# A two-layer hybrid encoder: the gate products issued in attention units 8 to 73 instead of 8 to 54

## The chip, the cores and the metric

The kernel runs on one core of one Trainium2 chip. The metric is the device time of one execution in microseconds (us), the median of several runs. A core has five engines with queues of their own: PE (TensorE, matmuls; its weight loads are shown as PEld), DVE (VectorE), ACT (ScalarE), POOL (GpSimd) and SP (SyncE, which only issues DMAs here). Each executes its own instructions in order and waits on semaphores for the others.

## What is computed

Two layers of an encoder on x of 1024 tokens by 1024 channels. Cut to what matters here, one layer is:

```
u  = RMSNorm(x) ;  z = u @ w_in          # q/k/v, two latents, a rotary key, and 2048 gate logits
yA = GQA(q, k, v)                        # 8 heads, 1024 queries x 1024 keys
yB = MLA(latent q, latent kv, rotary k)  # 8 heads, keys of width 96
g  = sigmoid(z_gate + b_gate)            # g_a and g_b
m  = (g_a * (yA @ w_branch_a) + g_b * (yB @ w_branch_b)) @ w_o
x  = x + RMSNorm(m) ;  x = x + RMSNorm(relu(RMSNorm(x) @ w_up)**2 @ w_down)
```

The gate logits need only u and w_in, so their product may stand anywhere between the projection and the branches. All products are made of two or three f16 matmuls (a high and a low part of each factor).

## The kernel before

**The attention stage.** After the projections, `mixer` runs one hand-written loop over 128 units per layer (s_ = 0 to 127, and a few more to drain). A unit is one head and one block of 128 queries against all 1024 keys. Units 0 to 63 are GQA, 64 to 127 MLA. On each engine the instructions stand in the order in which the loop writes them, except on SP, whose DMAs are placed by the framework. In unit s_ the loop writes, in this order: the rest of a gate group if it can be ended (`gate_matmuls(left)`) and its evacuation (`gate_out`, ACT); `bias(s_)` (DVE, line 828: scores times a factor, with a running minimum); the "low part" operations left from the unit before (`later`); the evacuation of the last preparation product (`prep_evac`); `low(s_-3)` (DVE); for every second unit `norm` and `high` (POOL and ACT); `expo(s_)` (ACT, exponential); `scores(s_+1)` (PE); a step of the weight tasks (`advance`); the transposes of a preparation (`prep_trans`); a part of the product with v (`av_part`, line 873, 24 matmuls); the gate matmuls due (`gate_matmuls(want)`, line 673); a preparation product (`prep_mm`, 15 matmuls on lines 318 to 320, which makes q, k and v of one MLA head pair for 128 tokens); one or two more steps of the weight tasks.

**Buffers.** Scores lie in PSUM tiles A (two of them), so PE may write the scores of unit s_+1 only when `expo(s_-1)` has read its own. Everything else that PE writes in this stage lies in PSUM tiles B (four): a gate group, an `av` sum, a preparation product, transposed pieces. In SBUF there are 28 tiles "m" of 4 KB a partition (activations, results, MLA's q and k) and four tiles "w" (weights split in two).

**The gates.** There are 768 matmuls of 128x512 in 32 groups of 24, two groups for each of 16 blocks of 128 gate channels. `want` spreads them linearly over units NQ = 8 to GS = 54. A block's weights are a task of their own: a 512 KB load, a sum of squares (ACT), a matmul with ones (PE, line 243) whose result DVE copies (line 245), then the high half (POOL, line 122) and the low half (DVE, line 137). With GD = 2 the halves may be written once the gates have come within two blocks of theirs. Tasks run one after another.

**What else hangs on the numbers.** The activations U (eight tiles m) are in use as long as gates are outstanding. `PRE` says in which units the four MLA preparations run (start, step); `QS` when their weights are loaded. YA and YB hold the two branches' results in halves of two tiles m each.

Of the kernel before, what the change touches and what calls it, by code (L numbers as in the profile page):

```python
# [9 lines left out]
F16 = mybir.dt.float16  # L10
# [34 lines left out]
def tile_hybrid_encoder(  # L45
# [13 lines left out]
    V, S, G, TE, SY = nc.vector, nc.scalar, nc.gpsimd, nc.tensor, nc.sync  # L59
    depth = w_in.shape[0]  # L60
# [4 lines left out]
    dr = ctx.enter_context(tc.tile_pool(name="dr", bufs=1, space=DRAM))  # L65
# [3 lines left out]
    def nm(s):  # L69
        cnt[0] += 1  # L70
        return f"{s}_{cnt[0]}"

    def mt(shape, dt=F16):
        return sb.tile(shape, dt, tag="m", name=nm("m"), bufs=NM)
# [190 lines left out]
    def both():  # L265

        halves = []

        def alloc(shape):
            if not halves:  # L270
                t = wt([128, 2, *shape[1:]])
                halves.extend((t[:, 0], t[:, 1]))
            return halves.pop(0)
        return alloc
# [38 lines left out]
    def kview(w, k0, nk, c0, n):  # L313

        return w[k0 * 128 : (k0 + nk) * 128, c0 : c0 + n].rearrange("(k p) n -> p k n", p=128)

    def mm3(o, lh, ll, rh, rl, first, last):
        TE.matmul(o, lh, rh, start=first, stop=False)  # L318
        TE.matmul(o, lh, rl, start=False, stop=False)  # L319
        TE.matmul(o, ll, rh, start=False, stop=last)  # L320

    x1 = [dr.tile([1024, D], F32, tag=f"x1{i}", name=f"x1{i}") for i in range(depth)]
    x2 = [dr.tile([1024, D], F32, tag=f"x2{i}", name=f"x2{i}") for i in range(depth - 1)] + [out]
    gates_d = [dr.tile([16, 128, 1024], F32, tag=f"gd{i}", name=f"gd{i}") for i in range(depth)]

    def first_weights(l, res):
# [32 lines left out]
    def mixer(l, U, su_inv, b2u, w_in_, rest, late, wnext):  # L359
# [211 lines left out]
        def q_end(cb, tb):  # L571
            q_live[cb, tb] = rope_end(*q_live[cb, tb])
# [34 lines left out]
        with tc.manual_schedule(engines=ENGINES):  # L607
            pre = prelims()
            for u in range(UN):
                evac = None  # L610
                if u < 16:
                    f, tb = units[u]
# [49 lines left out]
        NGM = 32 * 24  # L662
# [24 lines left out]
        def gate_weights(nb):  # L687
            wg.append([])
            yield from wprep_steps([kview(wi, 0, 8, 1440 + nb * 128, 128)], both(), wg[nb], 1,
                                   lambda: gate_pos[0] >= 48 * (nb - GD), GP)  # L690

# [23 lines left out]
        mla, wcache, prep = {}, {}, {}  # L715
# [20 lines left out]
        def mla_qweights(i):  # L736
            w = []
            yield from wprep_steps([kview(w_q_up[l], 0, 3, i * 192, 192)], both(), w)
            (h,), (lo,), inv, f2 = w
            b2, s, iq, cq = sm(), lay(1), lay(1), lay(1)  # L740
            mul(b2, f2, bounds[2])
            yield 1
            pow2(b2, 1, s, iq)
            yield 1
            mul(cq, inv, icq)
            ts(rsc[:, i, :], rc[:, :8], cq, ALU.mult, s, ALU.mult)
            yield 1
            kap = lay(2)
            mul(kap[:, 0:1], iq, wcache["kv"][3])
            ts(kap[:, 1:2], kap[:, 0:1], -1.0 / math.sqrt(96.0), ALU.mult)  # L750
            ts(kap[:, 0:1], kap[:, 0:1], 1.0 / math.sqrt(96.0), ALU.mult)
            wcache["q", i] = (h, lo, kap)

        def prep_mm(pr, tb):
            kvh, kvl = wcache["kv"][:2]
            wqh, wql, kap = wcache["q", pr]
            if tb == 0:
                QK = {(th, hl): mt([96, 4, 512]) for th in range(2) for hl in range(2)}
                mla[pr] = (QK, mt([128, 2, 8, 128]), kap)
            th, c0 = tb // 4, (tb % 4) * 128  # L760
            pd = psD()
            for k in range(3):
                mm3(pd[:, :192], CQ[th, 0][:, k, c0 : c0 + 128], CQ[th, 1][:, k, c0 : c0 + 128],
                    wqh[:, k, :], wql[:, k, :], k == 0, k == 2)
            for k in range(2):
                mm3(pd[:, 192:448], CK[0][:, k, tb * 128 : (tb + 1) * 128], CK[1][:, k, tb * 128 : (tb + 1) * 128],
                    kvh[:, k, pr * 256 : (pr + 1) * 256], kvl[:, k, pr * 256 : (pr + 1) * 256], k == 0, k == 1)
            prep[pr, tb] = pd
# [37 lines left out]
        YA = [[mt([128, 2, 1024]) for hl in range(2)]]  # L806
        YB = []
# [10 lines left out]
        def scores(u):  # L818
            units.append(unit(u))
            pa = psA()  # L820
            units[u][0](pa)
            live[u] = pa
# [59 lines left out]
            later.append(lambda: stt(Y[pr // 2][1][:, pr % 2, q2 * 256 : (q2 + 1) * 256], pc[:, :256], 1.0 / PSC, o,  # L882
                                     ALU.mult, ALU.subtract))

        GS = 54
        TS = 3
        AL = 2
        NQ = 8
        GL = 2
        GP = True  # L890
        KVS = 36
        QS = (42, 56, 69, 86)
        GD = 2
        PRE = [(53, 1), (62, 2), (79, 1.6), (95, 1.6)]
        WN = (90, 108)
        CUT = (4, 4)
        GCUT = 2
        preps = {}
        for pr, (s0, ds) in enumerate(PRE):
            for tb in range(8):  # L900
                preps[int(s0 + tb * ds)] = (pr, tb)
        wtasks = {KVS: mla_weights} | {s0: (lambda i=i: mla_qweights(i)) for i, s0 in enumerate(QS)}
        wtasks = {k: [v] for k, v in wtasks.items()}
        for nb in range(16):
            at = max(2 * nb, NQ + (nb - 2) * 48 * (GS - NQ) // NGM - GL)
            wtasks.setdefault(at, []).append(lambda nb=nb: gate_weights(nb))
        running, tiny = [], []

# [9 lines left out]
        with tc.manual_schedule(engines=ENGINES):  # L918
            scores(0)
            for s_ in range(NU + TS + AL + 2):  # L920
                want = min(NGM, max(0, NGM * (s_ + 1 - NQ) // (GS - NQ))) - gate_pos[0]
                left = 24 - gate_pos[0] % 24
                ended = None
                if 0 < left <= want:
                    ended = gate_pos[0] // 24
                    gate_matmuls(left)
                    want -= left
                if ended is not None:
                    gate_out(ended)
                if s_ < NU:  # L930
                    bias(s_)
                    tick()
                lows = list(later)
                later.clear()
                for f in lows:
                    f()
                if s_ - 1 in preps:
                    prep_evac(*preps[s_ - 1])
                if 0 <= s_ - 2 < 8:
                    q_end(1, s_ - 2)  # L940
                if 0 <= s_ - 1 < 8:
                    q_evac(1, s_ - 1)
                if s_ - 3 in (3, 7):
                    tiny.append(q_kappa(1, (s_ - 3) // 4))
                if 0 <= s_ - TS < NU:
                    low(s_ - TS)
                    tick()
                tick()
                while pend:
                    av_out(*pend.pop())  # L950
                pair = 0 <= s_ - 1 < NU and s_ % 2 == 0
                if pair:
                    norm(s_ - 1)
                    high(s_ - 1, G)
                if s_ < NU:
                    expo(s_)
                if pair:
                    high(s_ - 2, S)
                if s_ + 1 < NU:
                    scores(s_ + 1)  # L960
                advance()
                if s_ in (32, 64, 96):
                    (YA if s_ == 32 else YB).append([mt([128, 2, 1024]) for hl in range(2)])
                if s_ - 2 in preps:
                    prep_trans(*preps[s_ - 2])
                if av:
                    av_part(*av.pop(0))
                if 0 <= s_ - TS - AL < NU and (s_ - TS - AL) % 4 == 3:
                    pc = psC()
                    av += [((s_ - TS - AL) // 4, part, pc) for part in range(2)]  # L970
                if UN - QT + s_ < 8:
                    q_trans(0, UN - QT + s_)
                if 0 <= s_ - 3 < 8:
                    q_trans(1, s_ - 3)
                gate_matmuls(want)
                if s_ < 8:
                    q_mm(1, s_)
                if s_ in preps:
                    prep_mm(*preps[s_])
                if s_ in wtasks:  # L980
                    running += [w() for w in wtasks[s_]]
                running += [wnext[i](CUT[i]) for i in range(2) if s_ == WN[i]]
                for _ in range(min(len(running), 2)):
                    advance()
            while pend:
                av_out(*pend.pop())
            for f in later:
                f()
            for r in running:
                for _ in r:  # L990
                    pass
# [527 lines left out]
    for l in range(depth):  # L1519
        hold, wup0 = {}, [[], []]  # L1520
        YA, ivA, YB, ivB = mixer(l, U, su_inv, b2u, w1, first if l == 0 else None, late, mid_weights(l, hold))
# [75 lines left out]
```

## Time and profile before

| | us |
|---|---|
| median of 3 runs (lowest, highest) | 3160.08 (3155.36, 3162.07) |
| profiled execution, its own time | 3164.37 |
| its span, first to last instruction | 3162.6 |
| attention loop, layer 1 (first `bias` to the 128th) | 146.6 to 726.5 |
| attention loop, layer 2 | 1713.1 to 2293.6 |
| of it with gates, units 8 to 53, in each layer | 248.2 |

Busy time says what share of a stretch an engine spent on instructions; a matmul's shown duration runs past the start of the next one, so what a matmul costs in a dense run is read from the distance between starts. A stretch here begins and ends at the start of a `bias` row (line 828, one per unit): 146.6 is unit 0 of the first layer, 194.5 unit 8, 442.7 unit 54, 520.2 unit 73, 582.4 unit 90; in the second layer 1713.1, 1761.1, 2009.3, 2087.9 and 2147.5.

### The profile page before, as it was taken

Reading aid. Unit: us, or ns where it says so; the run is one execution under the profiler, and the core shown is the slowest. Engines: PE = TensorE matmul, PEld = TensorE weight load, DVE = VectorE, ACT = ScalarE, POOL = GpSimd, SP = SyncE. Lnnn points to the kernel's source line nnn. Section 1 sums busy time; section 2 is a strip of 40 time slices with the busy share of each in tenths; the row PEclk is TensorE's granted clock in tenths of the full one; section 3 lists DMA queues with packets and bytes.
Section 4 is the critical chain, followed back from the end, with each engine's and each line's share of the span. In section 5 each row is a group of like instructions: output and inputs, shape, how many; then the busy total and the mean of one; then the engine's idle time right before and its main releaser. Section 6 shows DMA issues by size and latency. Waiting matters only on the chain. (4 is left out here: it accounts for less than half of the span.)

```text
span 3162.6 us, 45495 instructions
## 1 busy us (share of the span) xinstructions
PE 2971.9 (94%) x17458; PEld 1588.4 (50%) x17458; DVE 1812.3 (57%) x3694; ACT 1507.3 (48%) x2326; POOL 598.2 (19%) x1037
## 2 busy tenths in 40 slices
PE   7989998778999999999999999988799999999998
PEld 5754455544454444444467545565444444444443
DVE  7676678885653333324767756798856533333155
ACT  4454557665444333324444545676654433333351
POOL 3341235640000000000224311466300000000002
PEclk9999999989999999999999999998899999999999
DMA  4057767776321111111410567687763211111112
GB/s 150 15 124 167 171 147 154 159 169 181 120 107 67 54 40 54 54 40 67 135 53 24 140 161 167 140 164 159 176 180 122 85 67 54 41 54 54 41 60 80
DMA packets 676410, 331.74 MB, mean 105 GB/s; under 512 B 555200, under 2 KB 634592, under 8 KB 676192
## 3 DMA queue, kind: packets, MB, share of 16 engines
q1 hardware_dynamic: 676192, 328.83, 40.0%
q8 instruction: 137, 2.24, 0.3%
q14 instruction: 81, 0.66, 0.1%
HBM read 160.97 MB, written 33.55 MB: 62 GB/s over the span
## 5 line engine op out<-in xcount | busy, mean ns | idle before, releaser
L1302 PE MATMUL A<-pt,m 128*128 128x512 f16 x2484 | 543.9, 379 | 1.6 <-DVE m L137 1.6
L1183 PE MATMUL A<-m,w 128*128 128x512 f16 x2496 | 544.3, 379 | 0.0
L1302 PEld LDWEIGHTS <-m 128*128 128x128 f16 x3072 | 300.7, 99 | 357.2 <-issue 1.8
L1183 PEld LDWEIGHTS <-w 128*128 128x128 f16 x2496 | 244.4, 99 | 288.0
L137 DVE SCALAR_TENSOR_TENSOR g<-p,sm,g 128x1024 f16<-128x1024 f32 x256 | 329.7, 1288 | 38.5 <-DMA pt<-g 19.2
L673 PE MATMUL B<-m,w 128*128 128x512 f16 x1536 | 348.2, 380 | 0.0
L140 ACT ACTIVATE m<-A,lay 128x1024 f32<-128x1024 f32 (+1 forms) x72 | 70.0, 972 | 444.0 <-PE A L1183 438.0
L319 PEld LDWEIGHTS <-m 128*128 128x128 f16 (+1 forms) x1728 | 172.3, 100 | 213.5 <-issue 123.9
L319 PE MATMUL A<-m,m 128*128 128x512 f16 (+3 forms) x704 | 261.1, 371 | 1.0 <-DVE m L125 1.0
L137 DVE SCALAR_TENSOR_TENSOR m<-A,lay,m 128x1024 f32<-128x1024 f32 x95 | 121.6, 1282 | 243.7 <-PE A L1302 243.7
L320 PE MATMUL A<-m,m 128*128 128x512 f16 (+3 forms) x704 | 260.8, 370 | 0.0
L318 PE MATMUL A<-m,m 128*128 128x512 f16 (+3 forms) x576 | 208.3, 362 | 54.2 <-ACT p L140 36.0
L122 POOL TENSOR_SCALAR g<-p,sm 128x1024 f16<-128x1024 f32 x128 | 152.2, 1189 | 525.1 <-DVE sm L843 388.3
L673 PEld LDWEIGHTS <-w 128*128 128x128 f16 x1536 | 147.7, 99 | 175.3 <-issue 8.6
L320 PEld LDWEIGHTS <-m 128*128 128x128 f16 (+1 forms) x1728 | 172.7, 100 | 121.9 <-issue 15.1
L318 PEld LDWEIGHTS <-m 128*128 128x128 f16 (+1 forms) x1728 | 173.3, 100 | 120.0 <-issue 21.3
L873 PE MATMUL B<-pt,m 128*64 128x256 f16 x3072 | 207.2, 287 | 6.5 <-DVE m L137 4.6
L140 ACT ACTIVATE p<-A,sm,lay 128x1024 f32<-128x1024 f32 x128 | 154.1, 1204 | 99.0 <-DVE p L828 90.5
L125 DVE TENSOR_TENSOR m<-B,m 128x512 f16<-128x512 f32 (+3 forms) x208 | 127.3, 634 | 121.3 <-ACT m L140 120.3
L873 PEld LDWEIGHTS <-m 128*64 128x64 f16 x3072 | 166.7, 115 | 56.1 <-issue 40.5
L137 DVE SCALAR_TENSOR_TENSOR w<-st,lay,w 128x2048 f16<-128x2048 f32 (+2 forms) x78 | 136.9, 1758 | 101.1 <-ACT w L140 63.3
L140 ACT ACTIVATE p<-A,sm,kq 128x1024 f32<-128x1024 f32 x128 | 153.9, 1202 | 85.1 <-DVE p L828 72.5
(166 smaller groups left out, 4791.5 us busy)
## 6 DMA issues: line engine op xcount, KB each, us to landing
st<-in_w_ffn_up_dram SPq DMA_DIRECT2D x32, 1024.0 KB, 5.3
st<-in_w_ffn_down_dram SPq DMA_DIRECT2D x32, 1024.0 KB, 4.9
st<-in_w_in_dram SPq DMA_DIRECT2D x32, 512.0 KB, 4.0
gd<-g SPq DMA_DIRECT2D x64, 256.0 KB, 2.5
p<-gd SPq DMA_DIRECT2D x64, 256.0 KB, 4.3
pt<-g SPq DMA_TRANSPOSE x512, 2.8
st<-in_w_o_dram SPq DMA_DIRECT2D x8, 1024.0 KB, 6.0
x<-p SPq DMA_DIRECT2D x16, 512.0 KB, 2.8
```

Of the source, the lines that this page charges most:

```text
L122: e.tensor_scalar(out=o, in0=i, scalar1=s1, scalar2=s2, op0=op0, op1=op1)
L125: e.tensor_tensor(out=o, in0=a, in1=b, op=op)
L137: V.scalar_tensor_tensor(out=o, in0=a, scalar=s, in1=b, op0=op0, op1=op1)
L140: S.activation(o, i, f, **k)
L318: TE.matmul(o, lh, rh, start=first, stop=False)
L319: TE.matmul(o, lh, rl, start=False, stop=False)
L320: TE.matmul(o, ll, rh, start=False, stop=last)
L673: TE.matmul(gate_live[g], lw, U[k // 4, th, (0, 1, 0)[v]][:, k % 4, :], start=(i == 0), stop=(i == 23))
L873: TE.matmul(pc[64 * i : 64 * i + 64, :256], VT[:, v, c, vc : vc + 64], PTs[g, i][p][:, c, :], start=(c == 0 and v == 0 and p == 0), stop=( ...
L1183: TE.matmul(pa[:, i * 512 : (i + 1) * 512], lw, U[k // 4, th, r][:, k % 4, :], start=(k == 0 and a == 0 and r == 0), stop=(k == 7 and a == 1))
L1302: TE.matmul(pa if pa.shape[1] == 512 else pa[:, n * 512 : (n + 1) * 512], a, r[k // 2][:, k % 2, n * 512 : (n + 1) * 512], start=(first an ...
```

## The change

The gates end at unit 73 (`GS = 73`) instead of 54. Since U then lives longer and the weights of the first MLA preparation fall into the same units, room is made: the first preparation's v tiles come from the four tiles w instead of m; the second halves of YA, the first of YB and the second of YB are taken later (units 38, 74, 102 instead of 32, 64, 96); the finished first half of YA (two tiles of 512 KB) is stored to DRAM in unit 42 and loaded again in unit 110. `GD = 1` lets a block's halves be written only one block ahead. The second preparation runs in units 69 to 76, one per unit, instead of 62 to 76, every second unit; its weights are loaded at 61 instead of 56, the third's at 72 instead of 69.

```diff
+    ya_d = [dr.tile([2, 128, 2048], F16, tag=f"yd{i}", name=f"yd{i}") for i in range(depth)]
...
-                mla[pr] = (QK, mt([128, 2, 8, 128]), kap)
+                mla[pr] = (QK, (wt if pr == 0 else mt)([128, 2, 8, 128]), kap)
...
-        GS = 54
+        GS = 73
...
-        QS = (42, 56, 69, 86)
-        GD = 2
-        PRE = [(53, 1), (62, 2), (79, 1.6), (95, 1.6)]
+        QS = (42, 61, 72, 86)
+        GD = 1
+        PRE = [(53, 1), (69, 1), (79, 1.6), (95, 1.6)]
...
-            at = max(2 * nb, NQ + (nb - 2) * 48 * (GS - NQ) // NGM - GL)
+            at = max(2 * nb, NQ - 1 + (nb - GD) * 48 * (GS - NQ) // NGM - GL)
...
-                if s_ in (32, 64, 96):
-                    (YA if s_ == 32 else YB).append([mt([128, 2, 1024]) for hl in range(2)])
+                if s_ in (38, 74, 102):
+                    (YA if s_ == 38 else YB).append([mt([128, 2, 1024]) for hl in range(2)])
+                if s_ == 42:
+                    for i, t in enumerate(YA[0]):
+                        SY.dma_start(out=ya_d[l][i], in_=t.rearrange("p a b -> p (a b)"))
+                if s_ == 110:
+                    YA[0] = [mt([128, 2, 1024]) for hl in range(2)]
+                    for i, t in enumerate(YA[0]):
+                        SY.dma_start(out=t.rearrange("p a b -> p (a b)"), in_=ya_d[l][i])
```

The lines behind the first added one stand one lower in the changed kernel, those behind the block at unit 42 eight lower.

First place: ACT early in the gates of the first layer. A row that reads `nbg` evacuates an ended gate group, a row `p<-A` is a unit's exponential. Before, units 12 and 13:

```order
L140 ACTIVATE g_2738<-B_2679,nbg_1890,lay_2736 128x512
L140 ACTIVATE p_2742,sm_2762<-A_2703,sm_2741,kq_281 128x1024
L140 ACTIVATE g_2764<-p_2614,sm_2754 128x1024
L140 ACTIVATE g_2772,sm_2727<-st_2728 128x1024
L140 ACTIVATE g_2800<-B_2775,nbg_1890,lay_2736 128x512
L140 ACTIVATE p_2804,sm_2762<-A_2767,sm_2803,kq_281 128x1024
```

Now, units 14 to 16:

```order
L140 ACTIVATE g_2793<-B_2723,nbg_1892,lay_2791 128x512
L140 ACTIVATE p_2797,sm_2812<-A_2746,sm_2796,kq_283 128x1024
L140 ACTIVATE g_2814<-p_2690,sm_2804 128x1024
L140 ACTIVATE g_2822,sm_2786<-st_2787 128x1024
L140 ACTIVATE m_1894<-B_2722 128x256
L140 ACTIVATE p_2860,sm_2812<-A_2817,sm_2859,kq_283 128x1024
L140 ACTIVATE g_2896<-B_2848,nbg_1892,lay_2791 128x512
L140 ACTIVATE p_2900,sm_2915<-A_2867,sm_2899,kq_283 128x1024
```

Before, two units out of three end a gate group; now every second unit does, from unit 10 to unit 72. 23 of the 32 groups (552 matmuls) are ended by the start of unit 54, and 9 groups (216 matmuls) follow.

Second place: PE in unit 55 of the first layer, at the preparation product of that unit (lines 318 to 320; `[waits ...]` names the semaphores of engines waited for). Before:

```order
L699 MATMUL A_5312<-m_261,m_1919 128x512
L796 MATMUL B_5317<-ident,g_5217 96x128 [waits Pool_49]
L796 MATMUL B_5317<-ident,g_5217 96x128 x3
L318 LDWEIGHTS m_271 [waits DVE_49]
L318 MATMUL B_5323<-w_4733,m_271 128x192 [waits PE_49]
L319 LDWEIGHTS m_271
```

Now:

```order
L674 MATMUL B_4970<-m_83,w_4666 128x512
L674 LDWEIGHTS w_4666
L674 MATMUL B_4970<-m_85,w_4666 128x512
L674 LDWEIGHTS w_4666
L674 MATMUL B_4970<-m_86,w_4666 128x512
L674 LDWEIGHTS w_4666
L674 MATMUL B_4970<-m_85,w_4666 128x512
L318 LDWEIGHTS m_273 [waits DVE_49]
L318 MATMUL B_5044<-w_4404,m_273 128x192 [waits PE_49]
```

A gate group (line 674 now) stands where none stood and holds one of the four tiles B. The wait for DVE is a wait for the tile: before, it is freed by DVE's low part of the product of unit 53, which DVE does behind the `bias` of unit 55; now by that of the product of unit 54, behind the `bias` of unit 56. Five preparation products per layer wait in this new way (units 55, 57, 58, 59 and 71). DVE's rows there are now, from the `bias` of unit 56 (line 829 now) on:

```order
L829 TENSOR_SCALAR p_5073,sm_5072<-A_5011,kq_283 128x1024
L137 SCALAR_TENSOR_TENSOR w_4873<-B_4974,rsc_281,w_4873 128x128
L137 SCALAR_TENSOR_TENSOR m_4035<-B_4815,m_4034 128x256
L125 TENSOR_TENSOR m_4870<-B_5026,m_4869 96x4x128
L137 SCALAR_TENSOR_TENSOR g_5090<-p_4822,sm_4926,g_4931 128x1024
```

The second of these rows frees the tile. Third place: POOL among the rotary steps of the first preparation in the first layer (rows on `sinb`, `cosb`, `kro`). Before, units 55 and 56:

```order
L122 TENSOR_SCALAR g_5295<-kro_277,lay_4396 128x32 x2
L125 TENSOR_TENSOR g_5295<-g_5295,sinb 128x2x8 x4
L125 TENSOR_TENSOR g_5295<-g_5295,cosb 128x2x32
L125 TENSOR_TENSOR g_5295<-g_5295 128x2x32
L122 TENSOR_SCALAR g_5345<-kro_277,lay_4396 128x32 x2
```

Now, units 56 and 57:

```order
L122 TENSOR_SCALAR g_5078<-kro_279,lay_4110 128x32 x2
L125 TENSOR_TENSOR g_5078<-g_5078,sinb 128x2x8 x4
L125 TENSOR_TENSOR g_5078<-g_5078,cosb 128x2x32
L125 TENSOR_TENSOR g_5078<-g_5078 128x2x32
L122 TENSOR_SCALAR g_5099<-p_4991,sm_5094 128x1024
L122 TENSOR_SCALAR w_5112<-st_4891,lay_5019 128x1024
L122 TENSOR_SCALAR g_5146<-kro_279,lay_4110 128x32 x2
```

The high half of a gate block (`w<-st`) now stands between rotary steps; three of the sixteen blocks do so or come later (units 56, 60 and 66), where before the last was written in unit 50.

## Rows read from the trace of the kernel before

**Rows 1.** The page, part 1: busy us, share of span, instructions.

```profile
PE 2971.9 (94%) x17458; PEld 1588.4 (50%) x17458; DVE 1812.3 (57%) x3694; ACT 1507.3 (48%) x2326; POOL 598.2 (19%) x1037
```

**Rows 2.** Busy time by stretch: stretch, length, PE, PEld, DVE, ACT, POOL, clock, DMA, GB/s.

```profile
146.60:194.50 47.90, 36.34 (x267) 27.90 (x266) 40.11 (x100) 27.15 (x50) 24.51 (x45) 0.94 0.35 78
194.50:442.70 248.20, 243.78 (x1520) 123.36 (x1520) 162.97 (x344) 126.37 (x193) 51.69 (x47) 1.00 0.72 162
442.70:520.20 77.50, 67.22 (x607) 47.82 (x606) 66.16 (x128) 56.52 (x112) 47.10 (x112) 0.96 0.60 135
520.20:582.40 62.20, 54.94 (x496) 37.06 (x495) 55.55 (x106) 46.17 (x90) 42.60 (x89) 1.00 0.82 163
...
1761.10:2009.30 248.20, 243.78 (x1519) 123.33 (x1519) 162.91 (x344) 126.34 (x193) 51.70 (x47) 1.00 0.69 162
2009.30:2087.90 78.60, 67.84 (x605) 48.67 (x604) 66.19 (x128) 56.61 (x112) 46.94 (x112) 0.93 0.69 130
2087.90:2147.50 59.60, 53.69 (x490) 36.40 (x489) 55.84 (x104) 45.84 (x90) 43.25 (x85) 1.00 0.87 171
```

**Rows 3.** PE in order of time, 328 to 345 us: start, duration, instructions.

```profile
327.94 5.34 PE L673 MATMUL B<-m,w 128*128 128x512 f16 x24
333.12 0.38 PE L698 MATMUL A<-m,m 128*128 128x512 f16 x1
...
334.08 1.50 PE L873 MATMUL B<-pt,m 128*64 128x256 f16 x24
335.51 0.61 PE L673 MATMUL B<-m,w 128*128 128x512 f16 x2
```

**Rows 4.** PE in order of time, 464 to 467 us (unit 58 to 59).

```profile
464.27 0.26 PE L318 MATMUL B<-w,m 128*128 128x192 f16 x1
...
465.68 0.38 PE L698 MATMUL A<-m,m 128*128 128x512 f16 x1
...
466.54 0.60 PE L796 MATMUL B<-ident,g 128*96 128x128 f32 x4
466.98 0.25 PE L318 MATMUL B<-w,m 128*128 128x192 f16 x1
```

**Rows 5.** PE by line, 442.7 to 520.2 us: count, busy, mean ns, idle before.

```profile
L873 PE MATMUL B<-pt,m 128*64 128x256 f16 x240 | 15.0, 275 | 2.6 <-DVE m L137 2.6
```

**Rows 6.** DVE by line, 194.5 to 442.7 us.

```profile
L137 DVE SCALAR_TENSOR_TENSOR w<-st,lay,w 128x1024 f16<-128x1024 f32 x14 | 18.0, 1282 | 17.7 <-POOL w L122 17.7
...
L245 DVE COPY lay<-B 128x1 f32<-128x1 f32 x16 | 2.5, 156 | 37.8 <-PE B L243 37.6
```

**Rows 7.** DVE by line, 442.7 to 520.2 us.

```profile
L828 DVE TENSOR_SCALAR_CACHE_REDUCE p<-A,kq 128x1024 f32<-128x1024 f32 x10 | 12.8, 1276 | 3.9 <-PE A L699 3.6
...
L125 DVE TENSOR_TENSOR m<-B,m 96x512 f16<-96x512 f32 x12 | 8.2, 681 | 3.5 <-ACT m L140 3.5
L137 DVE SCALAR_TENSOR_TENSOR m<-B,rsc,m 128x128 f16<-128x128 f32 x13 | 4.5, 346 | 0.0
...
L137 DVE SCALAR_TENSOR_TENSOR w<-st,lay,w 128x576 f16<-128x576 f32 x2 | 1.7, 836 | 0.0
```

**Rows 8.** Lines 125 and 137, 146.6 to 726 us: ns min/median/max, first and last start.

```profile
L125 POOL TENSOR_TENSOR g<-g,sinb x128: 213/220/1859, 446.1 to 658.4; 128x16 f32<-128x16 f32 x128
...
L137 DVE SCALAR_TENSOR_TENSOR g<-p,sm,g x124: 1264/1278/1405, 165.4 to 725.0; 128x1024 f16<-128x1024 f32 x124
```

**Rows 9.** The page, part 6: DMA issues, KB each, us from issue to landing.

```profile
st<-in_w_in_dram SPq DMA_DIRECT2D x32, 512.0 KB, 4.0
...
pt<-g SPq DMA_TRANSPOSE x512, 2.8
```

**Rows 10.** Waits, 520 to 726 us: total, times, longest.

```profile
PEld L873 <- DMA pt<-g: 1.9, 4, 1.1
```

## The prediction

> **What bounds the kernel now.** I read the page first, then the table by stretch, then PE and DVE by line inside the stretches. Over the whole span PE is busy 94% and DVE 57% [rows 1], but that is a mean over stages with different limits. In units 8 to 53, where the gates are, PE is busy 243.8 of 248.2 us (98.2%) and DVE 163.0: PE sets the pace and DVE idles 85.2 us. In units 54 to 72 nobody is full: PE 67.2, DVE 66.2 of 77.5 us; in units 73 to 89 PE 54.9, DVE 55.6 of 62.2. The second layer repeats all of it [rows 2]. So work that only PE needs lies in a stretch where PE is the bound, and next to it are stretches in which PE idles between waits. The change moves PE work from the one to the other. It can gain what PE idles there, and no more.
>
> **Prices.** In a dense run 24 gate matmuls take 333.12 - 327.94 = 5.18 us, 0.216 each; one part of the product with v takes 335.51 - 334.08 = 1.43 [rows 3]. A preparation product takes 465.68 - 464.27 = 1.41, a unit's GQA scores 0.86, four transposes 0.44 [rows 4]; MLA scores are six matmuls, 6 x 0.216 = 1.30. On DVE a gate block costs a low half of 1.28 and a copy of 0.16 [rows 6], 1.44 without its smallest operations; a preparation costs 0.35 + 0.68 = 1.03, the low half of an MLA weight 0.84 [rows 7].
>
> **Units 8 to 53.** By the order on ACT 9 of 32 gate groups, 216 matmuls, now come behind the start of unit 54: 216 x 0.216 = 46.7 us of PE leave, 243.8 - 46.7 = 197.1 stay. DVE loses three of the fourteen blocks that stand in this stretch [rows 6]: 163.0 - 3 x 1.44 = 158.7. How full PE can be with that is the main choice. With PE at 1.50 times DVE's work it is 98.2% full; where the two are level (1.02) the busier of them is 86.7%, 89.3%, 86.3% and 93.7% full in the four stretches behind the gates, mean 89.0% [rows 2]. The changed stretch has 197.1 / 158.7 = 1.24, and halfway between these points lies 93.3%: 211.3 us. The ends are 197.1 / 0.982 = 200.7 and 197.1 / 0.867 = 227.3. I take 211.3: 36.9 less than 248.2.
>
> **Units 54 to 72.** PE then has nine GQA scores (7.7), ten MLA scores (13.0), ten parts of the product with v (240 matmuls [rows 5], 14.3), eleven preparations (seven of the first, four of the second, 15.5), ten sets of transposes (4.4) and 216 gate matmuls (46.7): 101.6 us. DVE has 66.2 + 3 x 1.44 - 2 x 1.03 = 68.4, since two preparations move out to units 73 to 76. PE is at 1.49 times DVE's work, as in the gates' stretch before, so it is put at the same 98.2%: 103.5 us. The two layers took 77.5 and 78.6 [rows 2], mean 78.0: 25.5 more.
>
> **A wait that is added.** The gates hold one of the four tiles B. Five preparation products per layer now wait until DVE has done the `bias` of the next unit and the low part behind it: at most 1.28 + 0.35 = 1.63 us each [rows 7], 8.1 together; at least nothing. Behind the waiting product on PE are the next gate matmuls and the next scores, for which DVE's `bias` then waits. Ahead of it on PE, after the scores that `bias` reads, stand transposes and some ten gate matmuls, 0.44 + 10 x 0.216 = 2.6 us, which is more than 1.63. I take 0.3 each, 1.5 in all, with the ends 0 and 8.1 for the range.
>
> **Units 73 to 89 and 0 to 7.** Two more preparations and one MLA weight's low half come to units 73 to 89: 2 x 1.03 + 0.84 = 2.9 us of DVE, which is level with PE there and 89.3% and 93.7% busy [rows 2]: 2.9 / 0.915 = 3.2 more. One gate block is split behind unit 7 instead of before; DVE is the busiest there (40.1 of 47.9 us [rows 2]): 1.4 less.
>
> **Edits that I cost at nothing.** The two stores and two loads of 512 KB per layer. A 512 KB load lands 4.0 us after its issue and a transpose after 2.8 [rows 9]; were the transposes held up for the whole of each pair, 2 x 8 = 16 us per layer would be the upper end, and zero is the lower. SP's later transposes queue behind them, and the product with v waits for those; but it comes three units, over 9 us, behind the last transposed tile that it reads, and in units 73 to 127 it waited for transposes 1.9 us in all [rows 10]. The loaded half is read only by the branches, a dozen units later. If that cover failed, two pairs would show as waits of PE for DMA. The later units for YA and YB, and v tiles in w instead of m, issue no instruction; GD = 1 leaves a block's halves four units to be ready, some 18 us, for 1.28 us of DVE and about as much of POOL.
>
> **One rule weighed.** Three gate blocks now have their halves among or behind the rotary steps. In the trace a rotary step of POOL, 220 ns as a rule, reached 1859 ns, while DVE's low parts stayed between 1264 and 1405 ns [rows 8]: where the two meet, it is POOL that stands. The Trainium skill, SBUF — State Buffer (Who interferes with whom), says that a DVE instruction with two SBUF inputs and a POOL instruction that reads SBUF exclude each other for the whole instruction, and that whichever issues first wins. By that, if DVE were shut out by each of the three, the sum would be up to 3 x 1.28 = 3.8 us per layer worse; by the rows it is unchanged, as POOL is busy 47.1 of 77.5 us there [rows 2]. The trace agrees that one of them stands, with POOL's 1859 ns, and I stay with the rows.
>
> **The sum.** Per layer -36.9 + 25.5 + 1.5 + 3.2 - 1.4 = -8.1 us; two layers -16.2. All other instructions stand as before. The profiled execution took 3164.4 us (span 3162.6, 1.8 around it), so 3148.2 by its measure; the median of the runs is 4.3 lower, 3160.1, which gives **3144**.
>
> **Rivals.**
> (1) *The idle time fills completely.* The first stretch stays at 98.2%, 200.7 us, and the tile B wait costs nothing: -47.5 + 25.5 + 3.2 - 1.4 = -20.2 per layer, 3160.1 - 40.4 = 3120. For it: two A tiles let PE run ahead of DVE, and PE keeps 24% more work than DVE in every pair of units. Against it: no stretch with less surplus of PE work is over 94% full now [rows 2]. The Trainium skill, Perfetto Trace Analysis (Optimization Strategy), says that where the most contended engine changes over time, interleaving such regimes may improve performance; this rival is what that gives in full.
> (2) *DVE's waits stay, and it becomes the bound: slower.* For each gate block DVE copies a sum out of PSUM that PE makes behind all that is queued there (37.6 us of waiting in units 8 to 53) and waits for POOL's high half (17.7) [rows 6]. I assume that these waits shrink as PE's queue does. If instead DVE's 85.2 idle us shrink only with the blocks, by 11/14 to 67, the first stretch takes 158.7 + 67 = 225.7: -22.5 + 25.5 + 1.5 + 3.2 - 1.4 = +6.3 per layer, **3173**. It decides from 248.2 - 28.8 = 219.4 on, that is from 61 us of DVE waits. Against it: most of these waits are PE's surplus seen from DVE.
> (3) *The four B tiles cost their full price.* 8.1 instead of 1.5: -1.5 per layer, 3157, which is no measurable change. For it: DVE often lags in these units, where PE already waited for it to free such a tile [rows 5].
>
> **How the numbers follow.** The forecast gets 0.48, with its own range 3130 to 3160 from the ends of the first stretch; rival (1) 0.18, (2) 0.20, (3) 0.14. A measurement of this kernel can tell about 0.2%, 6.3 us, from no change: faster is below 3153.8, slower above 3166.4. Of the forecast's chance three quarters lie below and almost all the rest between; (1) is faster, (2) slower with a little between, (3) mostly between. Faster 0.36 + 0.18 + 0.01 = 0.55, no change 0.24, slower 0.21. The range reaches from just above (1) to just below (2), 3122 to 3172.
>
> **What would show it.** In the changed profile units 8 to 53 should last about 211 us with PE at 93%, units 54 to 72 about 104 with PE nearly full, units 73 to 89 three us more than before. PE waiting for `expo` or DVE waiting for line 243 over 60 us in units 8 to 53 would mean (2); PE idle before lines 318 to 320, ended by DVE, over 6 us per layer in units 54 to 72 means (3). Waits of PE for transposes behind units 42 and 110 would show that the stores and loads are not hidden. The prediction is wrong if units 8 to 53 take over 219 us, or if anything outside units 0 to 89 moves.

## The result, and the profile after

The changed kernel took 3206.95 us (median of 4 runs, 3205.44 to 3208.41), the kernel before 3161.07 beside it: a ratio of 1.0149, 95% interval 1.0131 to 1.0166. It is 46 us slower, where 16 us faster was forecast. The attention stages are 22.7 and 18.4 us longer in the profiled execution (602.6 and 598.9 from the first `bias` to the 128th). What lies ahead, between and behind them moved by -0.6, -1.4 and +4.2 us; the last also varies among the kernels below, by about as much, so the loss is looked for in attention.

The busy time by stretch of the changed kernel, with columns as in [rows 2]; the stretches are cut at the starts of `bias` (line 829 now): units 8 to 53, 54 to 72 and 73 to 89 of layer 1, then of layer 2.

```profile
192.49:406.44 213.95, 200.60 (x1322) 102.91 (x1320) 158.23 (x326) 117.98 (x180) 48.05 (x45) 0.98 0.75 176
406.44:532.43 125.99, 112.53 (x740) 63.87 (x738) 67.98 (x134) 58.38 (x111) 39.81 (x93) 0.92 0.50 116
532.43:604.93 72.50, 64.91 (x572) 45.78 (x572) 60.65 (x115) 52.97 (x106) 48.79 (x111) 0.95 0.73 137
...
1780.15:1995.88 215.73, 202.11 (x1320) 103.67 (x1319) 158.38 (x326) 117.86 (x180) 48.07 (x45) 0.98 0.77 175
1995.88:2121.66 125.78, 110.79 (x740) 62.83 (x738) 67.80 (x134) 58.28 (x111) 38.79 (x93) 0.95 0.52 116
2121.66:2189.31 67.65, 61.12 (x554) 43.17 (x553) 60.56 (x115) 52.60 (x106) 47.35 (x106) 0.97 0.68 146
```

The page's part 1 (columns as in [rows 1]) says that the work is the same, instruction for instruction:

```profile
PE 2987.0 (93%) x17458; PEld 1589.2 (50%) x17458; DVE 1813.2 (57%) x3694; ACT 1505.8 (47%) x2326; POOL 586.3 (18%) x1037
```

Against [rows 2], units 8 to 53 fell by 34.3 and 32.5 us, about as forecast (36.9). Units 54 to 72 grew by 48.5 and 47.2, not by 25.5, and units 73 to 89 by 10.4 and 8.0, not by 3.2. The loss is in these two stretches, most of it in the first. The granted clock says what kind of loss it is. It has two levels, 1.2 and 2.4 GHz, so a mean of 0.92 over 126.0 us is 16% of the time, 20.2 us, at the lower one, which costs half of that, 10.1 us, if PE works through it. PE's 112.5 busy us are then 102.4 us of work at full clock, 10.1 us of slow clock, and 13.5 us of standing come on top. In layer 2 it is 104.5, 6.3 and 15.0. The work is what the prediction added up (101.6). Standing still and a slow clock are what it left out. PE had stood 10.3 and 10.8 us in these units before [rows 2]; with the moved work it stands 13.5 and 15.0, so none of the idle time that was to be filled was filled.

The waits of three engines in units 54 to 72 of layer 1 (engine, line waited at <- released by: us in total, times, the longest):

```profile
ACT g L140 <- PE B L674: 48.7, 8, 9.5
...
DVE w L137 <- POOL w L122: 18.8, 3, 9.3
DVE lay L245 <- PE B L243: 10.6, 2, 7.1
...
PE B L797 <- DVE w L137: 7.8, 2, 3.9
PE B L797 <- DVE lay L245: 2.0, 2, 1.0
```

In these units of the kernel before, ACT waited for no gate product and DVE for no high half, and PE waited 1.6 us for such a low part of DVE (4.0 in layer 2). The first, second and fourth row belong to one chain. It is read best in unit 60, in order of time (start, duration, what was done, idle before and its releaser), engine by engine: PE, ACT, POOL, DVE, and PE again.

```profile
449.06 4.44 PE L674 MATMUL B<-m,w 128*128 128x512 f16 x12
...
454.62 0.27 PE L320 MATMUL B<-m,m 128*128 128x256 f16 x1
454.73 2.32 PE L674 MATMUL B<-m,w 128*128 128x512 f16 x10
...
457.09 0.78 ACT L140 ACTIVATE g<-B,nbg,lay 128x512 f32<-128x512 f32 x1 [7.24 <-PE B L674]
457.77 0.67 ACT L140 ACTIVATE g<-B,rsc 128x192 f32<-128x192 f32 x2
...
458.26 0.76 POOL L125 TENSOR_TENSOR g<-g,sinb 128x16 f32<-128x16 f32 x4 [7.92 <-ACT g L140]
...
459.80 1.12 POOL L122 TENSOR_SCALAR g<-p,sm 128x1024 f16<-128x1024 f32 x1
460.90 1.12 POOL L122 TENSOR_SCALAR w<-st,lay 128x1024 f16<-128x1024 f32 x1
461.99 1.52 POOL L122 TENSOR_SCALAR g<-kro,lay 128x32 f32<-128x32 f32 x2
...
462.05 1.30 DVE L137 SCALAR_TENSOR_TENSOR w<-st,lay,w 128x1024 f16<-128x1024 f32 x1 [9.30 <-POOL w L122]
463.28 1.27 DVE L829 TENSOR_SCALAR_CACHE_REDUCE p<-A,kq 128x1024 f32<-128x1024 f32 x1
464.48 0.34 DVE L137 SCALAR_TENSOR_TENSOR w<-B,rsc,w 128x128 f16<-128x128 f32 x1
...
460.66 0.38 PE L700 MATMUL A<-m,m 128*128 128x512 f16 x1
464.97 1.06 PE L797 MATMUL B<-ident,g 128*96 128x128 f32 x4 [3.93 <-DVE w L137]
```

PE makes 22 gate products that end a group. ACT reads the group out (`gate_out`, the row with `nbg`) and waits 7.24 us for it. The read-out of the preparation product (`prep_evac`, the row with `rsc`) stands behind it on ACT, though PE had that product ready since about 454.9 (line 320). POOL's rotary steps wait for that read-out, 7.92 us; the high half of the next gate block stands behind them on POOL. DVE's low half of that block waits for it, 9.30 us, and ahead of the next `bias`, so the `bias` of unit 61 starts late and the low part behind it, which frees a tile B, too. By then PE has run out of what it may do and stands 3.93 us. PE's products hold up the other three engines, then the three hold up PE: they take turns where they should overlap. Unit 60 is the longest of the stretch, 14.5 us; unit 56, 12.6 us, has the same chain with 3.92 us of standing. These two are the 7.8 us of the row `PE B L797 <- DVE w L137`.

### The profile page after: what moved, and what is told of

Same layout as the page of the kernel before. It is cut to its first block, busy times and chain, and to the rows that moved or that the text cites. A ratio compares the mean times of both kernels' runs of the same rounds, so it can differ in the third digit from the quotient of the medians.

```text
span 3205.9 us, 45453 instructions
## 1 busy us (share of the span) xinstructions
PE 2987.0 (93%) x17458; PEld 1589.2 (50%) x17458; DVE 1813.2 (57%) x3694; ACT 1505.8 (47%) x2326; POOL 586.3 (18%) x1037
## 5 line engine op out<-in xcount | busy, mean ns | idle before, releaser
L674 PE MATMUL B<-m,w 128*128 128x512 f16 x1536 | 369.4, 390 | 0.0
L137 DVE SCALAR_TENSOR_TENSOR g<-p,sm,g 128x1024 f16<-128x1024 f32 x256 | 329.1, 1286 | 41.3 <-ACT g L140 16.9
L137 DVE SCALAR_TENSOR_TENSOR m<-A,lay,m 128x1024 f32<-128x1024 f32 x95 | 121.6, 1282 | 245.0 <-PE A L1310 245.0
L318 PEld LDWEIGHTS <-m 128*128 128x128 f16 (+1 forms) x1728 | 172.8, 100 | 122.6 <-issue 18.0
L137 DVE SCALAR_TENSOR_TENSOR w<-st,lay,w 128x2048 f16<-128x2048 f32 (+2 forms) x78 | 136.9, 1758 | 153.8 <-POOL w L122 90.3
L140 ACT ACTIVATE p<-A,sm,kq 128x1024 f32<-128x1024 f32 x128 | 154.1, 1204 | 122.6 <-DVE p L829 90.1
L874 PE MATMUL B<-pt,m 128*64 128x256 f16 x2688 | 186.5, 293 | 1.7 <-DMA pt<-g 1.7
L829 DVE TENSOR_SCALAR_CACHE_REDUCE p<-A,lay 128x1024 f32<-128x1024 f32 x128 | 163.4, 1277 | 31.6 <-PE A L320 26.6
```

What stands on the lines that cost most here:

```text
L137: V.scalar_tensor_tensor(out=o, in0=a, scalar=s, in1=b, op0=op0, op1=op1)
L140: S.activation(o, i, f, **k)
L674: TE.matmul(gate_live[g], lw, U[k // 4, th, (0, 1, 0)[v]][:, k % 4, :], start=(i == 0), stop=(i == 23))
L829: V.tensor_scalar(out=P, in0=live[u], scalar1=units[u][1][:, 1:2], scalar2=None, op0=ALU.mult, op1=ALU.min, accum_out=nb)
L874: TE.matmul(pc[64 * i : 64 * i + 64, :256], VT[:, v, c, vc : vc + 64], PTs[g, i][p][:, c, :], start=(c == 0 and v == 0 and p == 0), stop=( ...
```

## The experiments

Theory A: the chain runs over ACT's order, where the read-out of a gate group stands ahead of the preparation's. Theory B: it runs over the gate weights; POOL makes a block's high half only when a w tile is free, and DVE's low half waits ahead of the `bias`. A third possibility was that the rest of the change, not the spread gates, costs the time. Lengths are layer 1 / layer 2 in us, ratios are to the kernel before in the same session (3160.8 to 3161.3 us). The stretches are those of one profiled execution of each kernel; two kernels with the same code in a stretch differ there by up to 3.8 us (before and e12 in units 73 to 89 of layer 2).

| kernel | median | ratio (95%) | units 8-53 | 54-72 | 73-89 |
|---|---|---|---|---|---|
| before | 3161.1 | | 248.2/248.2 | 77.5/78.6 | 62.1/59.7 |
| after | 3207.0 | 1.0149 (1.0131-1.0166) | 214.0/215.7 | 126.0/125.8 | 72.5/67.6 |
| e1_gs54 | 3167.3 | 1.0018 (1.0009-1.0028) | 247.3/248.7 | 75.1/73.9 | 68.9/66.0 |
| e2_gout | 3181.1 | 1.0059 (1.0043-1.0076) | 217.4/218.9 | 114.6/110.3 | 67.6/67.7 |
| e7_low | 3177.5 | 1.0053 (1.0038-1.0068) | 214.2/210.1 | 113.6/114.4 | 72.9/67.5 |
| e6_gout_low | 3166.4 | 1.0019 (1.0009-1.0028) | 215.4/211.7 | 107.6/113.1 | 68.5/67.7 |
| e5_nw5 | 3206.2 | 1.0144 (1.0125-1.0164) | 213.3/215.4 | 122.6/127.3 | 72.6/67.4 |
| e4_pause | 3158.1 | 0.9987 (0.9978-0.9996) | 216.2/219.0 | 100.2/99.6 | 71.8/67.9 |
| e8_pause_gout | 3153.9 | 0.9974 (0.9965-0.9984) | 220.4/216.6 | 98.5/97.7 | 69.2/68.3 |
| e9_all | 3157.6 | 0.9988 (0.9979-0.9998) | 218.6/215.5 | 110.2/109.9 | 61.3/61.0 |
| e10_spill | 3160.2 | 0.9995 (0.9986-1.0004) | 247.3/247.3 | 75.9/78.0 | 60.8/59.9 |
| e11_prep | 3174.2 | 1.0039 (1.0027-1.0052) | 247.3/248.5 | 78.4/77.3 | 66.6/65.8 |
| e12_bgout | 3152.4 | 0.9971 (0.9959-0.9982) | 243.7/243.7 | 77.5/75.8 | 60.8/63.5 |

**e1_gs54: the changed kernel without the spread.**

```diff
-        GS = 73
+        GS = 54
-        GD = 1
+        GD = 2
-            at = max(2 * nb, NQ - 1 + (nb - GD) * 48 * (GS - NQ) // NGM - GL)
+            at = max(2 * nb, NQ + (nb - 2) * 48 * (GS - NQ) // NGM - GL)
```

> The changed kernel with the gate products back in units 8 to 53 (and their weights prepared two blocks ahead); preparation 1 one per unit from unit 69, the low half in a w tile, the spill and the later tiles stay. If the spreading costs the time, units 54 to 72 fall back to about 78 + 4 us a layer and the kernel runs 3155 to 3180 us. If the rest of the change costs it, it stays at 3190 to 3207 us.

3167.3 us. Of the 46 us the rest of the change holds 6, the spread, with its `GD = 1`, 40. Units 54 to 72 were expected at about 82 us; they are even 2.5 and 4.7 us shorter than before, since two preparation products and three sets of transposes have left them, and units 73 to 89 are 6.8 and 6.4 longer.

**e2_gout: the read-out of a gate group behind the exponential.**

```diff
-                if ended is not None:
-                    gate_out(ended)
                 if s_ < NU:
                     bias(s_)
...
                 if s_ < NU:
                     expo(s_)
+                if ended is not None:
+                    gate_out(ended)
```

> The changed kernel with ScalarE's read-out of a finished gate group moved behind the exponential of its unit; the work is the same. Theory A (ScalarE's order: the read-out waits up to 9.5 us for TensorE's gate products, 48.7 us a layer in units 54 to 72, and the preparation's read-out, POOL, the block's halves and VectorE stand behind it): units 54 to 72 fall from 126 to 104-112 us a layer, the kernel runs 3165 to 3185 us. Theory B (the tiles of the gate weights: POOL makes a block's high half only when TensorE is done with the block two before, and VectorE waits behind POOL): units 54 to 72 stay at 120 to 126, 3195 to 3210 us.

3181.1 us, 26 less than the changed kernel: within theory A's range for the time; of units 54 to 72 (114.6 and 110.3, expected 104 to 112) one layer is beyond it. ACT's and DVE's waits in that stretch of layer 1:

```profile
ACT g L140 <- PE B L320: 25.1, 8, 5.8
...
ACT g L140 <- PE B L674: 4.0, 4, 2.5
...
DVE w L137 <- POOL w L122: 14.7, 3, 7.6
```

ACT no longer waits for the gate group (48.7 before the edit, 4.0 now). It waits for the preparation product instead, which PE makes behind gate products. DVE still stands 14.7 us behind POOL. One link was opened and the other is left.

**e7_low: the other link alone.** The low half of a gate block goes into the list that DVE works off behind the next `bias`.

```diff
-            if i:
+            if i and ready:
+                st, h, lo = parts[i - 1]
+                defer.append(lambda st=st, h=h, lo=lo: stt(lo, st, s, h, ALU.mult, ALU.subtract))
+            elif i:
...
-                                   lambda: gate_pos[0] >= 48 * (nb - GD), GP)
+                                   lambda: gate_pos[0] >= 48 * (nb - GD), GP, defer=later)
```

> The changed kernel with only the low half of a gate block moved behind the next bias; ScalarE's order as changed. If ScalarE's order is the first cause by itself, units 54 to 72 stay at 120 to 126 us a layer: 3197 to 3210 us. If VectorE's wait for POOL is a cause beside it, whichever comes first, they fall to 108 to 118: 3172 to 3192 us.

3177.5 us, 29.5 less than the changed kernel and within the second range. ACT's wait is still there and DVE's is gone (lines stand three lower), PE no longer waits for DVE's low part ahead of its transposes, and that suffices for more than half of the loss:

```profile
ACT g L140 <- PE B L677: 46.2, 8, 7.4
...
DVE w L137 <- POOL w L122: 0.8, 1, 0.8
```

So ACT's order is not the first cause by itself: with DVE's link open, ACT's wait of 46 us a layer is worth 11 us in both layers together, by the next run.

**e6_gout_low: both links.** The edits of e2 and e7 together.

> ScalarE's read-out of a finished gate group behind the exponential, as in the run before, and also VectorE's low half of a gate block behind the next unit's bias instead of ahead of it. If VectorE's standing behind POOL's high half (14.7 us a layer still) holds what was left, units 54 to 72 fall from 110-115 to 102-107 us a layer: 3158 to 3172 us. If the remainder is held by something else (the B tiles of the preparation, the copies of the sums of squares), they stay at 108 to 115: 3174 to 3184 us.

3166.4 us, 40.6 less. The two edits alone gave 26 and 29.5, 55 together; that the sum is not reached fits two links of one chain. Units 54 to 72 of layer 1 and layer 2:

```profile
408.41:516.02 107.61, 103.55 (x746) 61.20 (x744) 67.85 (x136) 61.67 (x114) 46.35 (x101) 1.00 0.65 141
...
1973.18:2086.29 113.11, 107.09 (x746) 62.24 (x744) 67.98 (x135) 61.76 (x114) 45.34 (x101) 0.97 0.61 131
```

At full clock PE's work takes 103.55 us, and it stands 4.1; layer 2 keeps 6.0 us of standing and 3.4 of slow clock. The expected range was 102 to 107; layer 1 misses it by 0.6 us, layer 2 by 6.

**e5_nw5: a fifth w tile.** `NW = 5`, `NM = 27`.

> The changed kernel with five w tiles in place of four (and 27 m tiles in place of 28, for the room). Theory B: VectorE's waits for POOL's high half (18.8 us a layer in units 54 to 72) fall below 6, units 54 to 72 fall by 8 to 18 us a layer, 3172 to 3192 us. Theory A: no more than 3 us a layer, 3200 to 3210 us; a wait for one of the 27 m tiles would add to it.

3206.2 us, no change, and DVE waits for POOL as before:

```profile
DVE w L137 <- POOL w L122: 18.5, 3, 9.0
```

The tiles are not what POOL waits for. Theory B stands only in its second half: DVE's place in the queue, not the room in w.

**e4_pause: no gate products beside preparation 0.** Units 8 to 52 take 576 gate matmuls (12.8 a unit), units 61 to 72 take 192 (16 a unit).

```diff
-                want = min(NGM, max(0, NGM * (s_ + 1 - NQ) // (GS - NQ))) - gate_pos[0]
+                want = gate_target(s_ + 1) - gate_pos[0]
...
+        GT = [(8, 0), (53, 576), (61, 576), (73, 768)]
```

> The changed kernel with the gate products in units 8 to 52 (12.8 a unit) and 61 to 72 (16 a unit), none in 53 to 60, where a preparation step stands in every unit. If it takes a preparation step and gate products in the same unit to lose the time (theories A and B both), units 54 to 60 fall from 57 to 32-36 us, units 61 to 68 grow with the gate products there to 42-48 and 8 to 53 to 222-228: 3160 to 3180 us. If any gate products behind unit 54 cost it, units 61 to 72 (now 69 us a layer) grow by 12 us beyond that, and the kernel stays at 3195 to 3215 us.

3158.1 us, 49 less than the changed kernel, just below the kernel before and 2 below the expected range. Both links of the chain are in place here; the meeting with preparation 0 is gone, while preparation 1 still meets gate products in units 69 to 72. Units 54 to 72 also hold 24 gate matmuls fewer than in the changed kernel, 5.2 us of PE, which explains a fifth of their fall. Units 54 to 72 of layer 1:

```profile
407.71:507.87 100.16, 95.93 (x703) 56.82 (x701) 66.31 (x131) 56.39 (x107) 42.15 (x93) 1.00 0.65 139
```

ACT's and DVE's waits there:

```profile
ACT g L140 <- PE B L674: 26.4, 7, 6.2
...
DVE w L137 <- POOL w L122: 2.4, 1, 2.4
```

ACT still waits 26.4 us for gate groups, but PE stands 4.2 and its clock is full. Units 54 to 60 take 27.2 and 26.7 us, and units 8 to 53 216.2 and 219.0, both below what was expected; 61 to 68 take 48.7 with 128 gate products, 0.7 above it.

**e8_pause_gout: the pause and the moved read-out.**

> Gate products in units 8 to 52 and 61 to 72, none beside preparation 0, and the read-out of a finished group behind the exponential. ScalarE still waited 26 us a layer for gate products there in units 54 to 72, but TensorE stood only 4 us, so the read-out's place is worth at most 4 us a layer now: 3150 to 3160 us. If ScalarE's wait costs by itself, wherever it stands, some 10 us a layer come off: 3132 to 3142 us.

3153.9 us, 4 less than the pause alone, as the first theory says: the read-out is worth no more than PE stands.

**e9_all: everything together, preparation 1 back at every second unit.** The edits of e8 and e7, `NW = 5`, `NM = 27`, `PRE` (62, 2), `QS` 56 and 69.

> All together: no gate products in units 53 to 60, the read-out behind the exponential, the low halves behind the next bias, five w and 27 m tiles, and preparation 1 back at every second unit from 62 (its weights from unit 56). The pause gave 3158 us; preparation 1 at one per unit cost 4 and 2 us a layer with the gates at home, the other moves up to 4 a layer: 3140 to 3156 us. If preparation 1 beside 16 gate products a unit loses as preparation 0 beside 12 did, 3165 to 3185 us.

3157.6 us, 4 more than e8 and 1.6 above the first range. Units 73 to 89 are back at 61.3 and 61.0, so it is preparation 1 that had made them longer; but units 54 to 72 take it back with 12 us. Of these 4.1 are work, two preparation products and three sets of transposes; in layer 1 PE stands 7.3 us there instead of 3.6, 6.6 of it waiting for DVE to free B tiles, and the clock falls from 1.00 to 0.97.

**e10_spill, e11_prep: parts of the change on the kernel before.** e10 has only the DRAM tile, the stores, the loads and the three later allocations; e11 only `QS = (42, 61, 72, 86)` and `PRE` (69, 1).

> The kernel before with the spill and the reload of the first half of YA and the later allocation of the three result tiles alone. The prediction's step: the DMAs lie beside other work, 0 (0 to 16) us. If hidden: 3156 to 3166 us. If the rest of the change (3167 us with the gate products at home, 6 above before) is the spill's: 3164 to 3172 us.

> The kernel before with preparation 1 at one per unit from unit 69 and the query weights taken later, nothing else. The prediction's step is +3.2 us a layer in units 73 to 89; with the gate products at home and all of the rest of the change those units grew by 6.8 and 6.4 and units 54 to 72 fell by 2.5 and 4.7. If preparation 1 is all of that rest: 3164 to 3172 us; if it is the prediction's size and the time before unit 73 falls by as much: 3158 to 3164 us.

The stores and loads cost nothing (0.9995). Preparation 1 at one per unit costs 13 us by itself, 2 above the range, more than the 6 that the whole rest costs in e1. Part of that must come back from the other edits of e1 (the v tiles in w, the later allocations); which one, no run here tells. Of the 13 us the profiled execution shows 8 in the two attention stages; where the others lie is not shown.

**e12_bgout: the moved read-out on the kernel before.** The edit of e2.

> The kernel before with the read-out of a finished gate group behind the exponential. There ScalarE waits 69 us a layer for gate products in units 8 to 53, more than the 49 in units 54 to 72 of the changed kernel. If the place of the read-out costs only where a preparation step stands behind it: no change, 3156 to 3166 us. If every unit in which a group ends pays for it: 3130 to 3150 us.

3152.4 us, between the two ranges. ACT's wait of the kernel before, units 8 to 53 of layer 1:

```profile
ACT g L140 <- PE B L673: 69.3, 23, 5.7
```

Most of that wait lies beside PE's work; what it could cost PE is hardly more than the 4.4 us that PE stood in each layer (248.2 less 243.8). With the edit the stretch takes 243.7 us and PE stands 1.4:

```profile
193.74:437.47 243.73, 242.31 (x1516) 122.71 (x1517) 161.52 (x343) 128.21 (x194) 51.87 (x47) 1.00 0.72 165
```

My two theories were all or nothing. The gain, 4.5 us in this stretch of each layer, has the size of PE's idle time there and not of ACT's wait.

e8 and e12 are both faster than the kernel before, by 0.26% and 0.29%; between them the runs show no difference.

## Why the prediction was wrong, step by step

**The prices and the work** were right. 101.6 us of PE work were added up for units 54 to 72; e6 shows 103.55 at full clock, the changed kernel 102.4 and 104.5 once the clock is taken out.

**Units 8 to 53**: forecast 211.3 with PE 93.3% full, measured 214.0 and 215.7, by the same measure 92% and 91% (197.1 us of work). PE stood 13.4 and 13.6 us, where the forecast had 14.2; the 2.7 and 4.4 us that it lacks are about what a mean clock of 0.98 costs there (4.3). Right within that, and the point from which rival (2) decides (219.4) was not reached. DVE's wait for line 243, 37.6 in [rows 6], fell to 12.0 as assumed; its wait for POOL's high half, 17.7 there, rose to 25.4.

**Units 54 to 72**: this is the step that failed. The work was put at 98.2% because PE had 1.49 times DVE's work, "as in the gates' stretch before". It was 81% by that measure (101.6 of 126.0). The ratio of two engines' work says how far one could run ahead of the other if only these two were tied. In the gates' stretch before, ACT's read-out waits for gate products as well (69.3 us) and DVE's low half for POOL (17.7 [rows 6]), but PE stood only 4.4 us there. With a preparation step in the unit, PE's own next step hangs on ACT, POOL and DVE in a row, and the ratio says nothing about that. The term also had no upper end, though the busier engine was only 86 to 94% full in the stretches behind the gates [rows 2]; at 86.7% it would have been 117, and the sum +5.6 us a layer. The range, too, was not worked out: the ends of the first stretch, 200.7 and 227.3, give 3123 and 3176 with the other terms as they stand, not the 3130 to 3160 that the prediction calls its own range. Even these miss 3207.

**The added wait** was forecast at 1.5 us (0 to 8.1), before lines 318 to 320. Measured: 7.8 us before line 797 for the low part, 2.0 more for line 245 (2.1 in layer 2), before the preparation products on lines 318 to 320 none in layer 1 and 0.7 in layer 2. What was missing was not the tile but why DVE came late: the prediction let it come 1.63 us late, `bias` and low part, and it came up to 9.3 us late. e7 leaves the number of tiles as it is and takes this wait away.

**GD = 1 at nothing.** That it "leaves a block's halves four units to be ready" is right for PE, whose waits show none for them. It overlooks that an instruction with time to spare can still hold up those queued behind it. The prediction asked who waits for the halves, and not who is queued behind them. No run has `GD = 2` together with the spread, so what `GD` itself adds is not shown.

**The clock** was no term at all. It took 10.1 and 6.3 us in units 54 to 72, where before it took 3.1 (0.96) and 5.5 (0.93).

**Units 73 to 89**: forecast +3.2; +6.8 and +6.4 in e1, +10.4 and +8.0 in the changed kernel. The mechanism was right (e9 takes it away by moving preparation 1 back) and the size too small by half.

**Units 0 to 7** (-1.4; measured -1.3 and -1.6) and **the spill** (0; e10 measures 0.9995) were right.

**The rule weighed.** The Trainium skill, SBUF — State Buffer (Who interferes with whom), made POOL and DVE shut each other out, up to 3.8 us a layer if DVE lost. DVE's low halves in units 56 and 60 took 1.30 us beside POOL, where [rows 6] has 1.28; two small POOL steps beside each took 1.52 us, 0.56 in unit 59. So POOL stands, as the rows before said, and no run here shows DVE shut out.

**The rivals.** "Slower" was given to rival (2) alone, which put DVE's waits into units 8 to 53. The wait it named, DVE behind POOL's high half, was a link of the real chain, in units 54 to 72. The signs named for (2) and (3) did not appear: DVE waited 12.0 us for line 243 and not over 60, PE at most 0.7 before the preparation products and not over 6. But the 7.8 us before line 797 are nearly the full price that (3) put on the B tiles, 8.1; PE paid it at the transposes, and because DVE stood behind POOL.

What the spread is worth with the chain out of the way: e6, with both links open, is no faster than e1, which has no spread at all (1.0019 and 1.0018). In e6 PE stands 14.2 and 14.8 us in units 8 to 53 where it stood 4.4, so the gain that was to come from filling is used up by new standing there. Only the pause shows a gain, 9 us from e1 to e4. It pays for the rest of the change, and little is left: e8 is level with e12, which moves no gate product and takes away the standing in units 8 to 53 by the read-out's place alone. What PE waits for in units 8 to 53 is in the trace of the changed kernel, layer 1:

```profile
PE A L699 <- ACT p L140: 7.8, 7, 2.5
PE B L243 <- ACT g L140: 4.8, 3, 2.3
```

It is ACT, at the exponential and at the sums of squares of the gate weights; before, these two took 3.5 and 0.9 us. Why ACT comes later at 12 to 13 products a unit was not tried.

## What to carry to other kernels

Before work is moved into a stretch, follow for one of its units every instruction that will wait for the moved work, and on each engine the instructions queued behind it: a wait with time to spare becomes a link as soon as a neighbour in the queue is needed soon. A fill rate from one stretch holds in another only if the same engines are tied there within a unit; otherwise take the rates of the worse stretches as the other end. Read-outs and weight halves that nobody needs soon belong behind the steps that the bound engine waits for.

## What was not expected of the hardware

PE's granted clock fell after quite short stands. Rows of the changed kernel in unit 59 and early in unit 60 (columns as in [rows 2]):

```profile
446.00:448.00 2.00, 1.02 (x5) 0.39 (x3) 1.49 (x2) 2.00 (x7) 1.69 (x3) 1.00 0.76 174
448.00:449.00 1.00, 0.40 (x4) 0.43 (x5) 0.93 (x6) 0.75 (x2) 1.00 (x4) 1.00 0.80 178
449.00:450.00 1.00, 1.00 (x6) 0.49 (x5) 1.00 (x1) 0.59 (x1) 0.84 (x4) 0.82 1.19 273
450.00:451.00 1.00, 1.00 (x3) 0.30 (x2) 1.00 (x5) 0.00 (x0) 0.34 (x2) 0.50 1.47 114
...
453.00:454.00 1.00, 1.00 (x11) 0.77 (x10) 0.00 (x0) 0.00 (x0) 0.00 (x0) 0.98 0.91 204
```

PE was busy 1.42 of the 3 us from 446, in pieces with no single stand over 1 us. In 450 to 451 the clock is at its lower level, 1.2 GHz, and PE, by now with a full queue, works off gate products at half rate: the row of 12 at 449.06 lasts 4.44 us. In 453 to 454 it is back. During the 3.93 us of standing at the end of the unit it falls again, to a mean of 0.50 over the whole of unit 61 (463.28 to 466.74), and the four transposes at 464.97 take 1.06 us where those at 448.60 took 0.61.

How much the clock weighs is seen in e5, whose two layers run the same 740 matmuls with nearly the same waits:

```profile
405.41:527.97 122.56, 108.41 (x740) 62.77 (x738) 68.04 (x134) 58.15 (x111) 39.25 (x93) 0.96 0.51 119
1996.32:2123.60 127.28, 112.50 (x740) 63.73 (x738) 67.89 (x134) 58.40 (x111) 40.02 (x93) 0.92 0.52 115
```

0.04 of granted clock over some 125 us goes with 4.1 us more of PE's busy time. So a chain that makes PE stand is paid for twice: while it stands, and in the clock behind it.
